# Two-layer trunk on one core: fourteen chunks of the down projection as seven block products per pair, placed between the gate/up chunks

## Chip, core and metric

The kernel runs on one core of one Trainium2 chip. The time is device microseconds of one launch; several runs are timed and their median is given. Smaller is better.

## What is computed

A trunk of two layers on 256 tokens with 1024 features, in float32. Each layer is a gated token mixer and a SwiGLU feed-forward part, each followed by a LayerNorm of the scaled residual. The change lies in the feed-forward part:

```python
def swiglu(x, w_gate, w_up, w_down):
    return (jax.nn.silu(x @ w_gate) * (x @ w_up)) @ w_down

for l in range(DEPTH):                       # DEPTH = 2
    mix = hybrid_mixer(x, w_in[l], w_branch_sb[l], w_branch_moba[l], w_out[l])
    x = layer_norm(DEEPNORM_ALPHA * x + mix, ln_mix_g[l], ln_mix_b[l])
    ffn = swiglu(x, w_ffn_gate[l], w_ffn_up[l], w_ffn_down[l])
    x = layer_norm(DEEPNORM_ALPHA * x + ffn, ln_ffn_g[l], ln_ffn_b[l])
```

The hidden width is 2816, which is 22 chunks of 128. h is silu(gate) times up.

## The kernel before

**Precision by parts.** Every float32 operand is split into a rounded part `hi` and a rest `lo` (`x - hi`), and each product is three matmuls (`mm3`): hi by hi, hi by lo, lo by hi.

**Weights.** `WeightStream` brings the weights as granules of 128 x 1024 in the order in which TensorE uses them, 122 per layer (`NG_LAYER`). A granule is loaded by SyncE's queue into one of six `raw` buffers (`NRAW`), ScalarE casts it to `whi`, VectorE subtracts to `wlo`. Both parts go to rings of ten places (`NSPLIT`): granule g takes the place of g - 10, and `allow` lets it be written once TensorE is done with that. Seven granules per layer, all in the mixer (`SOFT_IN_LAYER`), go another way and are called soft: POOL's queue starts a rounding DMA straight into `whi` (`cast_line`), ScalarE writes its negative into `wlo`, and POOL's queue starts a DMA that adds the weights to it (`rest_line`).

**Feed-forward part.** In a layer granules 56 to 63 are gate and up for chunks 0 to 3, computed with the tokens as rows (`pft`, `h_line`). Granules 64 to 99 are gate and up for chunks 4 to 21, two per chunk (`feat_major`, tiles `pf`, 48 matmuls of 256 columns per chunk), into two PSUM banks in turn; after each chunk ScalarE and VectorE make h and split it (`swiglu_line`, tile `sf`). Granules 100 to 121 are the down projection, one per chunk (`token_out`, tiles `pd`, in layer 1 also `pe`): for each of two token blocks and two halves of 512 columns an `mm3`. Its first 14 chunks run for both token blocks, the last 8 (`HOLD`) first for one and then for the other, so that the first block's norm runs beside the second block's chunks.

**Order.** TensorE's order is that of the code. What ScalarE, VectorE and the queues do between is put in order while the program is written: `Weave` keeps an estimated clock for each engine, and side lines (`line`, `cast_line`, the h lines, the norms) are continued when their due time has come. Each engine then works through its list in that order and waits where an operand isn't there. `SOFT_LAND` is the landing time that this planner assumes for a soft granule.

Of the kernel before, what the change touches and what calls it, by code (L numbers as in the profile page):

```python
# [14 lines left out]
P = 128  # L15
# [15 lines left out]
NG_LAYER = 122  # L31
NTOK_FC = 4


# [65 lines left out]
class WeightStream:  # L100
# [5 lines left out]
    def __init__(self, nc, pool, rings, w, total, weave):  # L106
        self.nc, self.pool, self.rings, self.w, self.total, self.weave = nc, pool, rings, w, total, weave
        self.soft = [g for g in range(total) if SOFT(g)]
        self.hard = [g for g in range(total) if not SOFT(g)]
        self.loaded = self.split = self.cast = self.done = 0  # L110
        self.limit = NSPLIT - 1
# [7 lines left out]
    def open(self, g):  # L119

        self._open(g)
        self.parts[g] = [self._part(i, g) for i in range(2)]
        self.ready[g] = 0.0
        self.loaded = self.split = g + 1
# [4 lines left out]

    def moved(self, start, dst, g, **kw):  # L130

        b, i = divmod(g % NG_LAYER - 40, 4)
        if 0 <= b < 2:
            g += i - 4 * b
            start(dst.rearrange("p (c n) -> p c n", c=2),
                  self.w[g:g + 2, :, b * 512:(b + 1) * 512].rearrange("c p n -> p c n"), **kw)
        else:
            start(dst, self.w[ORDER.get(g, g)], **kw)

    def load(self, upto):  # L140

        while self.loaded < min(upto, len(self.hard)):
            g = self.hard[self.loaded]
            before = self.hard[self.loaded - NRAW] if self.loaded >= NRAW else None
            self._open(g)
            self.moved(self.nc.sync.dma_start, self.raw[g], g)
            self.dma_t = max(self.dma_t, self.ready.get(before, 0.0) + 0.5) + 1.46
            self.there[g] = self.dma_t + 1.0
            self.loaded += 1

    def _part(self, i, g):


        at = g % NSPLIT * GCOLS + (ON[i] if self._on(g) else 0)
        return self.rings[i][:, at:at + GCOLS]

    def _on(self, g):
        return any(a <= g < b for a, b in STATIONARY)

    def line(self):  # L160

        nc, weave = self.nc, self.weave
        while self.split < len(self.hard):
            g = self.hard[self.split]
            ahead = g - self.current
# [6 lines left out]
            self.load(self.split + NRAW)  # L172
            if ahead > 0:
                yield self.there[g]
            hi, lo = (self._part(i, g) for i in range(2))
            t = self.raw.pop(g)
            e = weave.act(self.there[g], GCOLS, nc.scalar.copy, hi, t)
            if g - self.current > 0:
                yield e
            e = weave.dve(e, GCOLS, nc.vector.tensor_sub, lo, t, hi.bitcast(F32))  # L180
            self.parts[g], self.ready[g] = (hi, lo), e
            self.split += 1
            self.load(self.split + NRAW)

    def cast_line(self):
        nc, weave = self.nc, self.weave
        while self.cast < len(self.soft):
# [6 lines left out]
            self.dma_t = max(self.dma_t, e + 1.0) + 2.2  # L194
            self.there[g] = self.dma_t + SOFT_LAND[self.weave.measured]
            self.cast += 1
# [23 lines left out]
    def allow(self, g):  # L220

        reaches = self._on(g) and not self._on(g - NSPLIT + 1) and g % NSPLIT < NSPLIT - 1
        self.limit = max(self.limit, min(g - reaches, self.total - 1))

# [22 lines left out]
NRAW = 6  # L247
SOFT_IN_LAYER = (22, 25, 28, 31, 34, 37, 40)


def SOFT(g):
    return g % NG_LAYER in SOFT_IN_LAYER


NSPLIT = 10
ON = (16, 48)
STATIONARY = ((8, 20), (24, 50), (64, 100), (130, 140), (146, 170), (186, 220))
HOLD = 8
TURNED = ("l0sb3", "l1sb3")
# [18 lines left out]
def hybrid_trunk_kernel(ctx: ExitStack, tc: tile.TileContext, w, xT_in, x_in, ln_in,  # L278
# [39 lines left out]
    def turn(e):  # L318

        was = None  # L320
        while True:
# [5 lines left out]
            else:  # L327
# [5 lines left out]
             for p, n, on in ((ring0, "whi", ON[0]), (ring1, "wlo", ON[1]))]  # L333
    ws = WeightStream(nc, wpool, rings, w, DEPTH * NG_LAYER, weave)
    act, dve, pool = weave.act, weave.dve, weave.pool
# [445 lines left out]

    def residual(e, x, cs, ps, sum_out=None):
        return dve(e, cs.stop - cs.start, nc.vector.scalar_tensor_tensor, x[:, cs], x[:, cs], ALPHA, ps,
                   op0=OP.mult, op1=OP.add, accum_out=sum_out)

# [9 lines left out]

    def norm_line(name, t, junk, gb):

# [27 lines left out]
    def last_norm(name, t, banks, gb, down):  # L825
# [8 lines left out]
        for i, (c0, ps) in enumerate(banks):  # L834
            if t == 1:
                down([(c0, ps)])
            residual(pe_done(), x, cols[i], ps)
            e = dve(0.0, cols[i].stop - c0, nc.vector.bn_stats, st[:, i, :], x[:, cols[i]])
# [16 lines left out]
    for l in range(DEPTH):  # L855
        G = l * NG_LAYER
        L = f"l{l}"
# [185 lines left out]
        hb = [unit(f"{L}hb{t}", [P, 2, 2, 256]) for t in range(2)]  # L1043
        h_t = [pair_tiles(f"{L}h0", [P, 4, S])]

        def h_parts(c):
            if c // 4 == len(h_t):
                h_t.append(pair_tiles(f"{L}h{c // 4}", [P, 4, S]))
            return h_t[c // 4][0][:, c % 4, :], h_t[c // 4][1][:, c % 4, :]

        def h_line(name, ps, j, t):
            sg = work.tile([P, 256], F32, tag="T", name=name)
            e = act(pe_done(), 256, nc.scalar.activation, sg, ps[:, :256], AF.Sigmoid)
            yield e
            dve(e, 256, nc.vector.tensor_mul, sg, sg, ps[:, :256])
# [3 lines left out]
            yield from split_line(*(blocked(h[:, 2 * j:2 * j + 2, ts]) for h in h_t[0]), tp, 256, e)  # L1059

        def swiglu_line(name, ps, hi, lo):
            sg = work.tile([P, S], F32, tag="T", name=name)
            e = act(pe_done(), S, nc.scalar.activation, sg, ps[:, 0, :], AF.Sigmoid)
            yield e
            dve(e, S, nc.vector.tensor_mul, sg, sg, ps[:, 0, :])
            e = dve(e, S, nc.vector.tensor_mul, sg, sg, ps[:, 1, :])
            yield e
            yield from split_line(hi, lo, sg, S, e)

        sides = []  # L1070
        for t in range(2):
            weave.finish(norms[:t + 1])
            pe_after(xT_ready[t])
            for j in range(2):
# [6 lines left out]
                sides.append(weave.start(h_line(f"{L}sg{t}{j}", ps, j, t)))  # L1081
        for c in range(NTOK_FC, NFC):
            ps = bankM(f"{L}pf{c}", [P, 2, S])
            for b in range(2):
                feat_major(ps[:, b, :], G + 56 + 2 * c + b)
            weave.start(swiglu_line(f"{L}sf{c}", ps, *h_parts(c)))
        weave.finish(sides)


        gb = load_gb(l, 1)  # L1090
        acc = [bankB(f"{L}pd{t}", [P, 2, 512]) for t in range(2 if l < DEPTH - 1 else 1)]
        banks = [[(512 * h, a[:, h, :]) for h in range(2)] for a in acc]
        if l == DEPTH - 1:
            banks.append([(0, bankM(f"{L}pe0", [P, 512])), (512, bankM(f"{L}pe1", [P, 512])[:, :256]),
                          (768, bankC(f"{L}pe2", [P, 512])[:, :256])])
        g = G + 100
        for c in range(NFC - HOLD):
            for t in range(2):
                token_out(banks[t], g + c, t, *h_parts(c), c == 0, False)
            ws.allow(g + NSPLIT + c)  # L1100
        norms = []
        for t in range(2):
            def down(part, t=t):
                for c in range(NFC - HOLD, NFC):
                    token_out(part, g + c, t, *h_parts(c), False, c == NFC - 1)
                    if t == 1:
                        ws.allow(g + NSPLIT + c)
            if l < DEPTH - 1:
                down(banks[t])
                norms.append(weave.start(norm_line(f"{L}b", t, acc[t], gb)))  # L1110
            else:
                last_norm(f"{L}b", t, banks[t], gb, down)
# [86 lines left out]
```

## Time and profile before

| | |
|---|---|
| runs timed | 718.47, 719.17, 720.03 us; median 719.17 us |
| span of the profiled execution | 716.7 us; a time of its own beside the span is not listed |
| TensorE (PE) busy | 708.0 us, 99%; mean clock granted 0.997 |
| VectorE (DVE) busy | 528.3 us, 74% |
| ScalarE (ACT) busy | 389.3 us, 54% |
| GpSimd (POOL) busy | 34.6 us, 5% |
| DMA | 157.84 MB, mean 220 GB/s |
| layer 0, gate/up chunks 4 to 21 | 198.1 to 296.0 us |
| layer 0, down projection | 296.0 to 356.9 us |
| layer 1, gate/up chunks 4 to 21 | 549.9 to 648.2 us |
| layer 1, down projection and last norm | 648.2 us to the end |

PE is the matmul unit, PEld its weight loads, which overlap. Names such as `whi<-raw` read output from input. Most instructions are recorded at a helper's line (L442 matmuls, L49 ScalarE, L54 VectorE, L59 POOL), so that tiles tell more than lines. Square brackets in a timeline hold the engine's idle time before an instruction and what ended it. Matmuls are pipelined: one lasts longer in the trace than the distance to the next.

### The profile page before, as it was taken

The page shows a single profiled execution, that of the slowest core. Times are in us where ns is not written, and L with a number is a line of the kernel's source. Part 1 is how long each engine was busy: PE and PEld are TensorE (multiplying, and loading weights), DVE is VectorE, ACT ScalarE, POOL GpSimd, SP SyncE. Part 2 cuts the span into 40 slices and gives each one's busy share as a digit, 9 for nine tenths or more (in the row PEclk, how much of TensorE's full clock was granted, in tenths as well). Part 3 has the DMA queues.
Part 4 walks back from the last instruction along what each step waited for, and adds up shares of the span by engine and source line. Part 5 has one row for each costly group of instructions (what it writes and reads, how often), then busy time and mean ns, then how long its engine had stood idle before and what let it go on. Part 6 is the DMA issues. An engine that isn't in the chain of part 4 may idle for free.

```text
span 716.7 us, 12727 instructions
## 1 busy us (share of the span) xinstructions
PE 708.0 (99%) x4981; PEld 651.0 (91%) x4981; DVE 528.3 (74%) x789; ACT 389.3 (54%) x582; POOL 34.6 (5%) x48
## 2 busy tenths in 40 slices
PE   9999999999999999999999999999999999999995
PEld 7889999998899999988889889999888999998885
DVE  5999887898987666643688888879889776665416
ACT  5766677754655545432365567676556554554300
POOL 0001110001000000000000111100010000000001
PEclk9999999999999999999999999999999999999998
DMA  8898889876596555385259589996748855553501
GB/s 291 342 332 248 244 235 252 288 272 228 197 306 231 181 204 196 128 313 187 85 175 347 160 218 242 242 292 207 260 166 282 302 185 196 191 202 99 225 1 59
DMA packets 63053, 157.84 MB, mean 220 GB/s; under 512 B 10896, under 2 KB 23184, under 8 KB 62992
## 3 DMA queue, kind: packets, MB, share of 16 engines
q1 hardware_dynamic: 58304, 142.07, 57.3%
q0 software_dynamic: 4544, 14.68, 9.0%
q8 instruction: 39, 0.64, 0.4%
q10 hardware_dynamic: 144, 0.26, 0.1%
q14 instruction: 22, 0.18, 0.1%
HBM read 148.87 MB, written 8.13 MB: 219 GB/s over the span
## 4 chain that ended last, share of the span: by engine, by line
PE 97%; DMA 1%; SPq 1%; DVE 0%; POOL 0%; POOLq 0%; issue 0%; ACT 0%; DVEq 0%
PE l1pf L442 14%; PE l0pf L442 14%; PE l0pd L442 8%; PE l0pg L442 6%; PE l1pg L442 6%; PE l1pe L442 4%; PE l1pd L442 4%; PE l1pqk L442 3%; PE l1pft L442 3%; PE l0pqk L442 3%; PE l0pw L442 3%; PE l1pvq L442 3%; PE l0pft L442 3%; PE l1pw L442 3%; PE l1pk L442 2%; PE l0pk L442 2%
## 5 line engine op out<-in xcount | busy, mean ns | idle before, releaser
L54 DVE TENSOR_TENSOR wlo<-raw,whi 128x1024 fp32r<-128x1024 f32 (+1 forms) x234 | 277.2, 1202 | 79.6 <-ACT whi L49 76.5
L49 ACT CAST whi<-raw 128x1024 fp32r<-128x1024 f32 (+1 forms) x233 | 237.5, 1036 | 81.5 <-PE l0pd L442 19.4
L442 PE MATMUL l1pf<-xT_hi,whi 128*128 128x256 f32 x288 | 79.6, 276 | 0.0
L442 PE MATMUL l1pf<-xT_hi,wlo 128*128 128x256 f32 x288 | 79.6, 276 | 0.0
L442 PE MATMUL l1pf<-xT_lo,whi 128*128 128x256 f32 x288 | 79.6, 276 | 0.0
L442 PE MATMUL l0pf<-xT_hi,wlo 128*128 128x256 f32 x288 | 79.5, 276 | 0.0
L442 PE MATMUL l0pf<-xT_hi,whi 128*128 128x256 f32 x288 | 79.5, 276 | 0.0
L442 PE MATMUL l0pf<-xT_lo,whi 128*128 128x256 f32 x288 | 79.5, 276 | 0.0
L442 PEld LDWEIGHTS l1pf<-xT_lo,whi 128*128 128x128 f32 x288 | 54.1, 188 | 0.0
L442 PEld LDWEIGHTS l1pf<-xT_hi,whi 128*128 128x128 f32 x288 | 54.1, 188 | 0.0
L442 PEld LDWEIGHTS l1pf<-xT_hi,wlo 128*128 128x128 f32 x288 | 54.1, 188 | 0.0
L442 PEld LDWEIGHTS l0pf<-xT_lo,whi 128*128 128x128 f32 x288 | 54.1, 188 | 0.0
L442 PEld LDWEIGHTS l0pf<-xT_hi,whi 128*128 128x128 f32 x288 | 54.1, 188 | 0.0
L442 PEld LDWEIGHTS l0pf<-xT_hi,wlo 128*128 128x128 f32 x288 | 54.1, 188 | 0.0
L442 PE MATMUL l0pg<-xT_hi,whi 128*128 128x256 f32 x128 | 35.7, 279 | 0.0
L442 PE MATMUL l1pg<-xT_hi,whi 128*128 128x256 f32 x128 | 35.6, 278 | 0.0
L442 PE MATMUL l0pg<-xT_hi,wlo 128*128 128x256 f32 x128 | 35.4, 277 | 0.0
L442 PE MATMUL l0pg<-xT_lo,whi 128*128 128x256 f32 x128 | 35.4, 277 | 0.0
L442 PE MATMUL l1pg<-xT_hi,wlo 128*128 128x256 f32 x128 | 35.4, 277 | 0.0
L442 PE MATMUL l1pg<-xT_lo,whi 128*128 128x256 f32 x128 | 35.4, 276 | 0.0
L442 PE MATMUL l0pd<-whi,l0h_hi 128*128 128x512 f32 x88 | 34.5, 391 | 0.0
L442 PE MATMUL l0pd<-wlo,l0h_hi 128*128 128x512 f32 x88 | 34.3, 389 | 0.0
(371 smaller groups left out, 1781.5 us busy)
## 6 DMA issues: line engine op xcount, KB each, us to landing
raw<-in_w_dram SPq DMA_DIRECT2D x226, 512.0 KB, 4.5
whi<-in_w_dram POOLq DMA_DIRECT2D x14, 512.0 KB, 6.2
wlo<-in_w_dram POOLq DMA_DIRECT2D x14, 512.0 KB, 8.2
ln<-in_ln_dram SPq DMA_DIRECT2D x8, 512.0 KB, 6.0
raw<-in_w_dram SPq DMA_DIRECT2D x7, 256.0 KB, 5.8
l0mb_scr<-l0mb_turn SPq DMA_DIRECT2D x4, 384.0 KB, 7.2
l0mb_turn<-l0mb_scr SPq DMA_DIRECT2D x16, 96.0 KB, 5.3
l1mb_scr<-l1mb_turn SPq DMA_DIRECT2D x4, 384.0 KB, 6.3
```

Of the source, the lines that this page charges most:

```text
L49: f(*args, **kw)
L54: f(*args, **kw)
L442: nc.tensor.matmul(o, a, b, start=start, stop=stop)
```

## The change

Chunks 4 to 17 of the down projection become seven pairs. A pair's work is a product of 2 x 2 blocks (two token blocks by two chunks, two chunks by two halves of the output columns), and it is done by seven block products in place of eight, with sums of blocks of h and of the weights made beforehand. Seven sums of products stay in PSUM over all pairs: `p1`, `p5`, `p6`, `p7` and three halves of `acc`. After pair 6 `combine_line` adds and subtracts them into x on VectorE, with the residual's factor; the norm then adds the tail's sums with factor 1.

Pair j (chunks 4+2j and 5+2j) stands between gate/up chunks: products with its first two granules, then gate/up chunk 8+2j, the other products, chunk 9+2j. Chunks 4 to 7 come ahead of pair 0, so h of a pair is made two pairs ahead. From chunk 8 on gate/up uses one PSUM bank (`single`, half of `acc[1]`) instead of two, since the products hold the others. Chunks 0 to 3 and 18 to 21 (`TAIL`) stay as before and come last, first for one token block and then for the other.

A pair has four weight granules from two loads: B11 (half a granule: the first 512 columns of the first raw buffer), B2X (the second raw buffer whole), T13 and T42 (sums made in place in the two raw buffers by four VectorE adds of 512 columns). A layer has 136 granules instead of 122; pair j has the eight granules 72+8j to 79+8j: B11, B2X, gate and up of a chunk, T13, T42, gate and up of the next. The up granule 75+8j is soft: seven more soft granules per layer, and the planner's landing time for them is 6 us. Silu replaces Sigmoid and a multiply, and ScalarE copies the up part from PSUM.

```diff
+NPROD = 7
+NS_LAYER = NG_LAYER + 2 * NPROD
+LEAD_FC = NTOK_FC + 4
+TAIL = [*range(NTOK_FC), *range(NTOK_FC + 2 * NPROD, NFC)]
...
-SOFT_IN_LAYER = (22, 25, 28, 31, 34, 37, 40)
+SOFT_IN_LAYER = (22, 25, 28, 31, 34, 37, 40, *(59 + 2 * LEAD_FC + 8 * j for j in range(NPROD)))
...
+            if kind == B11:
+                t = t[:, :512]
+            elif kind == T13:
+                u = self.raw[of + 1]
+                a, b = (slice(i * 512, (i + 1) * 512) for i in range(2))
+                dve = weave.dve
+                dve(max(e, self.there[of + 1]), 512, add, t[:, a], t[:, a], t[:, b])
+                e = dve(0.0, 512, add, t[:, b], t[:, b], u[:, b])
+            n = t.shape[1]
+            e = weave.act(e, n, nc.scalar.copy, hi, t)
+            if kind == T13:
+                dve(0.0, 512, add, u[:, b], u[:, b], t[:, a])
+                self.there[of + 1] = dve(0.0, 512, add, u[:, a], u[:, a], u[:, b])
...
+        def activated(name, ps):
+            both = work.tile([P, 512], F32, tag="T", name=name)
+            act(pe_done(), S, nc.scalar.activation, both[:, :S], ps[:, 0, :], AF.Silu)
+            e = act(pe_done(), S, nc.scalar.copy, both[:, S:], ps[:, 1, :])
+            return both, e
...
+        def product(o, j, h, w, i):
+            hi, lo = h_pair[j % 3]
+            cs = slice(i * 512, (i + 1) * 512)
+            mm3(o, hi[:, h, :], lo[:, h, :], w[0][:, cs], w[1][:, cs], j == 0, j == NPROD - 1 and h in (0, 2, 6, 7))
...
+        for j in range(NPROD):
+            weave.finish(made[2 * j:2 * j + 2])
+            pe_after(h_there[j])
+            w = ws.take(g)
+            product(p1, j, 0, w, 0)
+            ws.allow(g + NSPLIT)
+            w = ws.take(g + 1)
+            product(acc[0][:, 0, :], j, 4, w, 0)
+            product(acc[0][:, 1, :], j, 3, w, 1)
+            ws.allow(g + 1 + NSPLIT)
+            h_chunk(LEAD_FC + 2 * j, single, g + 2)
+            w = ws.take(g + 4)
+            product(p5, j, 6, w, 0)
+            product(p7, j, 2, w, 1)
+            ws.allow(g + 4 + NSPLIT)
+            w = ws.take(g + 5)
+            product(acc[1][:, 0, :], j, 5, w, 0)
+            product(p6, j, 7, w, 1)
+            ws.allow(g + 5 + NSPLIT)
+            if j == NPROD - 1:
+                combined = [weave.start(combine_line())]
+            h_chunk(LEAD_FC + 2 * j + 1, single, g + 6)
+            g += 8
...
-        for c in range(NFC - HOLD):
-            for t in range(2):
-                token_out(banks[t], g + c, t, *h_parts(c), c == 0, False)
-            ws.allow(g + NSPLIT + c)
```

**ScalarE in layer 0, around chunks 8 and 9.** The number behind `raw` is the granule; `l0sf8` is chunk 8's tile. Before, a chunk has one activation, its h cast and two weight casts:

```order
L49 ACTIVATE l0sf8_2628<-l0pf8_2563 128x256
L49 CAST whi_98<-raw83_2459 128x1024
L49 CAST l0h2_hi_2626<-l0sf8_2628 128x256
L49 CAST whi_98<-raw84_2476 128x1024
L49 ACTIVATE l0sf9_2691<-l0pf9_2630 128x256
L49 CAST whi_98<-raw85_2523 128x1024
L49 CAST l0h2_hi_2626<-l0sf9_2691 128x256
L49 CAST whi_98<-raw86_2541 128x1024
```

Now, beginning with T13 of the next pair (granule 84, in buffer `raw80`); `raw81` is granule 85, T42, and the activation from `whi` to `wlo` is the negation of soft granule 83:

```order
L54 CAST whi_98<-raw80_2283 128x1024
L54 ACTIVATE l0sf8_2645<-l0pd1_2564 128x256
L54 COPY l0sf8_2645<-l0pd1_2564 128x256
L54 CAST whi_98<-raw81_2424 128x1024
L54 CAST whi_98<-raw86_2458 128x1024
L54 CAST whi_98<-raw87_2488 128x1024
L54 ACTIVATE wlo_99<-whi_98 128x1024
L54 CAST whi_98<-raw88_2535 128x512
L54 ACTIVATE l0sf9_2731<-l0pd1_2564 128x256
L54 COPY l0sf9_2731<-l0pd1_2564 128x256
L54 CAST whi_98<-raw89_2655 128x1024
L54 CAST l0hp2_hi_2291<-l0sf8_2645 128x512
```

The negation stands behind the casts of granules 86 and 87; the activation and the copy of a chunk now read the one bank (`l0pd1`) that the next chunk writes.

**VectorE at the same place.** Before, a chunk has two multiplies with a PSUM operand and one subtraction of 256 columns beside two granules:

```order
L54 TENSOR_TENSOR wlo_99<-raw82_2407,whi_98 128x1024
L54 TENSOR_TENSOR l0sf8_2628<-l0sf8_2628,l0pf8_2563 128x256 x2
L54 TENSOR_TENSOR wlo_99<-raw83_2459,whi_98 128x1024
L54 TENSOR_TENSOR l0h2_lo_2627<-l0sf8_2628,l0h2_hi_2626 128x256
L54 TENSOR_TENSOR wlo_99<-raw84_2476,whi_98 128x1024
```

Now, from chunk 11 to the first granules after chunk 12:

```order
L59 TENSOR_TENSOR l0sf11_2894<-l0sf10_2811,l0sf11_2894 128x256
L59 TENSOR_TENSOR l0sf10_2811<-l0sf11_2894 128x128
L59 TENSOR_TENSOR wlo_99<-raw97_2794,whi_98 128x1024
L59 TENSOR_TENSOR l0hp0_lo_2288<-l0sf10_2811,l0hp0_hi_2287 128x512
L59 TENSOR_TENSOR l0hp0_lo_2288<-l0sf11_2894,l0hp0_hi_2287 128x512
L59 TENSOR_TENSOR wlo_99<-raw98_2830,whi_98 128x1024
L59 TENSOR_TENSOR raw96_2701<-raw96_2701 128x512
L59 TENSOR_TENSOR raw96_2701<-raw96_2701,raw97_2794 128x512
L59 TENSOR_TENSOR raw97_2794<-raw97_2794,raw96_2701 128x512
L59 TENSOR_TENSOR raw97_2794<-raw97_2794 128x512
L59 TENSOR_TENSOR wlo_99<-raw96_2701,whi_98 128x1024
L59 TENSOR_TENSOR l0sf12_2974<-l0sf12_2974 128x256
```

The four adds of raw weights and the sums of h are new in the list; nothing of a chunk's h reads PSUM any more.

**POOL in layer 0 after the mixer.** Before, nothing but the norms' small operations:

```order
L59 TENSOR_TENSOR l0a_ve1_2091<-l0a_ve1_2091,mhalf_105 128x1
L59 TENSOR_SCALAR l0b_ve0_3743<-l0b_ve0_3743 128x1
L59 TENSOR_TENSOR l0b_ve0_3743<-l0b_ve0_3743,mhalf_105 128x1
L59 TENSOR_SCALAR l0b_ve1_3834<-l0b_ve1_3834 128x1
L59 TENSOR_TENSOR l0b_ve1_3834<-l0b_ve1_3834,mhalf_105 128x1
```

Now the first of seven times two DMAs stand there:

```order
L64 TENSOR_TENSOR l0a_ve1_2091<-l0a_ve1_2091,mhalf_105 128x1
L146 DMA whi_98<-in_w_dram 128x1024
L146 DMA wlo_99<-in_w_dram 128x1024
L146 DMA whi_98<-in_w_dram 128x1024
L146 DMA wlo_99<-in_w_dram 128x1024
```

Each pair's rounding DMA is issued behind the adding DMA of the pair ahead of it.

More of the change, by code (lines that the diff above doesn't have):

```diff
@@ L109, in __init__ @@
         self.hard = [g for g in range(total) if not SOFT(g)]
+        self.loads = [g for g in self.hard if SLOTS[g][0] in (FULL, B11, B2X)]
         self.loaded = self.split = self.cast = self.done = 0
+        self.freed = {}
         self.limit = NSPLIT - 1
@@ L128, in load_piece, with moved @@
         self.dma_t += 0.73
-    def moved(self, start, dst, g, **kw):
+    def moved(self, start, dst, slot, **kw):
+        g = SLOTS[slot][1]
         b, i = divmod(g % NG_LAYER - 40, 4)
@@ L138, in moved, with load @@
             start(dst, self.w[ORDER.get(g, g)], **kw)
[L140 to L144, printed above, removed]
+    def load(self, upto=None):
+        while self.loaded < min(upto or len(self.loads), len(self.loads)):
+            g = self.loads[self.loaded]
+            before = self.loads[self.loaded - NRAW] if self.loaded >= NRAW else None
+            if before is not None and before not in self.freed:
+                break
             self._open(g)
             self.moved(self.nc.sync.dma_start, self.raw[g], g)
-            self.dma_t = max(self.dma_t, self.ready.get(before, 0.0) + 0.5) + 1.46
+            self.dma_t = max(self.dma_t, self.freed.get(before, 0.0) + 0.5) + 1.46
             self.there[g] = self.dma_t + 1.0
@@ L151, in _part, with _place @@
     def _part(self, i, g):
[L154 to L158, printed above, removed]
+        kind = self._place(g)
+        at = g % NSPLIT * GCOLS + (ON[i] if kind == "on" else HALF_AT if kind == "half" else 0)
+        return self.rings[i][:, at:at + (512 if kind == "half" else GCOLS)]
+    def _place(self, g):
+        if SLOTS[g][0] == B11:
+            return "half"
+        if SLOTS[g][0] == B2X:
+            return "off"
+        return "on" if any(a <= g < b for a, b in STATIONARY) else "off"
     def line(self):
         nc, weave = self.nc, self.weave
+        add = nc.vector.tensor_add
         while self.split < len(self.hard):
             g = self.hard[self.split]
+            kind = SLOTS[g][0]
             ahead = g - self.current
@@ L171, in line @@
                 continue
-            self.load(self.split + NRAW)
-            if ahead > 0:
+            self.load()
+            of = g - 4 if kind in (T13, T42) else g
+            if ahead > 0 and of == g:
                 yield self.there[g]
             hi, lo = (self._part(i, g) for i in range(2))
-            t = self.raw.pop(g)
-            e = weave.act(self.there[g], GCOLS, nc.scalar.copy, hi, t)
+            t = self.raw[of]
+            e = self.there[of]
+            if kind == B11:
[11 more added lines that the diff above has]
+                self.there[of + 1] = dve(0.0, 512, add, u[:, a], u[:, a], u[:, b])
             if g - self.current > 0:
                 yield e
-            e = weave.dve(e, GCOLS, nc.vector.tensor_sub, lo, t, hi.bitcast(F32))
+            e = weave.dve(e, n, nc.vector.tensor_sub, lo, t, hi.bitcast(F32))
             self.parts[g], self.ready[g] = (hi, lo), e
+            if kind in (FULL, T13, T42):
+                self.raw.pop(of)
+                self.freed[of] = e
             self.split += 1
-            self.load(self.split + NRAW)
+            self.load()
     def cast_line(self):
@@ L220, in allow @@
     def allow(self, g):
-        reaches = self._on(g) and not self._on(g - NSPLIT + 1) and g % NSPLIT < NSPLIT - 1
-        self.limit = max(self.limit, min(g - reaches, self.total - 1))
+        g = min(g, self.total - 1)
+        reaches = self._place(g) == "on" and self._place(g - NSPLIT + 1) == "off" and g % NSPLIT < NSPLIT - 1
+        self.limit = max(self.limit, g - reaches)
     def reach(self, g):
@@ new lines, in hybrid_trunk_kernel, with combine_line @@
+        taken[0] += 2
+        p1, p6 = (bankC(f"{L}pd{n}", [P, 512]) for n in ("one", "six"))
+        p5, p7 = (bankM(f"{L}pd{n}", [P, 512]) for n in ("five", "seven"))
+        def combine_line():
+            e = pe_done()
+            u = work.tile([P, 512], F32, tag="T", name=f"{L}comb")
+            e1 = act(e, 512, nc.scalar.copy, u, p1)
+            e = residual(e, xs[0], halves[0], p1)
+            left[turns[0]] = max(e, e1)
+            yield e1
+            left[turns[1]] = e = dve(e1, 512, nc.vector.tensor_add, u, u, p6)
+            residual(e, xs[0], halves[1], u, op=OP.subtract)
+            residual(e, xs[0], halves[1], p5, scale=1.0)
+            yield weave.dve_t + HOP
+            e = dve(e, 512, nc.vector.tensor_sub, u, u, p7)
+            residual(e, xs[1], halves[0], u)
+            yield weave.dve_t + HOP
+            residual(e, xs[1], halves[1], u, op=OP.subtract)
+            residual(e, xs[1], halves[1], p5, scale=1.0)
@@ L1101, in hybrid_trunk_kernel, with h_parts @@
+        def h_parts(i):
+            return [h[:, i % 4, :] for h in (h_tok, h_rest)[i // 4]]
         norms = []
```

119 lines of the change are left out of this document (80 added, 39 removed).

## The prediction

> **What bounds the kernel now.** I read the page's totals first, then the chain that ended last in order of time, then the busy time by stretches.
>
> ```profile
> span 716.7 us, 12727 instructions
> PE 708.0 (99%) x4981; PEld 651.0 (91%) x4981; DVE 528.3 (74%) x789; ACT 389.3 (54%) x582; POOL 34.6 (5%) x48
> PE 97%; DMA 1%; SPq 1%; DVE 0%; POOL 0%; POOLq 0%; issue 0%; ACT 0%; DVEq 0%
> ...
> 198.09 97.94 PE l0pf L442 x864
> 296.03 55.79 PE l0pd L442 x246
> ...
> 549.92 98.26 PE l1pf L442 x864
> ...
> 198.10:296.00 97.90, 97.90 (x865) 97.90 (x865) 68.46 (x96) 51.51 (x76) 0.00 (x0) 1.00 0.62 219
> ```
>
> TensorE carries 97% of the chain. Its pieces in layer 0's gate/up stage (l0pf) and down stage (l0pd) join without a gap. So whatever leaves TensorE's list is gained, and whatever makes TensorE wait is lost, one for one. A 256-column matmul costs 97.94/864 = 0.1134 us there, a 512-column one 55.79/246 = 0.2268 us, the same per column. The last row has the columns PE, PEld, DVE, ACT, POOL, clock, DMA share, GB/s: the clock is at 1.00, VectorE busy 70%, ScalarE 53%. The time outside the span is not listed for this execution; the runs' median, 719.17, is 2.5 above the span, and I keep that.
>
> **TensorE's sum.** Two chunks of the down projection cost 2 x 2 tokens x 2 halves x 3 = 24 matmuls of 512 columns. Seven products cost 21. Seven pairs in two layers save 7 x 2 x 3 = 42 x 0.2268 = 9.53 us. Chunks 0-3 and 18-21 keep 12 each, and gate/up keeps its count. The end of layer 1 keeps its last pieces (eight chunks, half by half), so nothing is lost there.
>
> **VectorE and ScalarE in a pair.** One pair's period on TensorE is 96 x 0.1134 + 21 x 0.2268 = 15.65 us. The prices are distances between starts, since neighbours overlap by some 0.1 us:
>
> ```profile
> 214.88 0.88 DVE L54 TENSOR_TENSOR l0sf<-l0sf,l0pf 128x256 f32<-128x256 f32 x2 [0.90 <-ACT l0sf L49]
> 215.82 1.23 DVE L54 TENSOR_TENSOR wlo<-raw,whi 128x1024 fp32r<-128x1024 f32 x1
> 216.96 0.42 DVE L54 TENSOR_TENSOR l0h_lo<-l0hb,l0h_hi 128x256 fp32r<-128x256 f32 x1
> ...
> 353.44 0.68 DVE L54 TENSOR_TENSOR xT_lo<-l0b_tp,xT_hi 128x512 fp32r<-128x512 f32 x1
> 354.04 1.22 DVE L54 TENSOR_TENSOR wlo<-raw,whi 128x1024 fp32r<-128x1024 f32 x1
> ...
> 369.37 0.29 DVE L54 TENSOR_TENSOR l1qmb_ra<-l1qmb_tok,rope 128x128 f32<-128x128 f32 x1 [1.08 <-ACT l1qmb_tok L49]
> ...
> 214.47 0.38 ACT L49 ACTIVATE l0sf<-l0pf 128x256 f32<-128x256 f32 x1 [1.74 <-PE l0pf L442]
> 214.75 1.04 ACT L49 CAST whi<-raw 128x1024 fp32r<-128x1024 f32 x1
> 215.69 0.40 ACT L49 CAST l0h_hi<-l0hb 128x256 fp32r<-128x256 f32 x1
> ```
>
> VectorE: six subtractions of 1024 columns at 1.14 (215.82 to 216.96) = 6.84; half a granule 0.60; the four adds of raw weights, each reading the one before, at their full 0.68 = 2.72; the h lines with two multiplies of 256 at 0.42, one subtraction of 256 at 0.42, two of 128 at 0.29, two of 512 at 0.60 = 3.04. Sum 13.2 of 15.65, 84%. ScalarE: six casts at 0.94 = 5.64, half a cast 0.5, a negation 0.94, two Silus and two copies at 0.28 = 1.1, two casts of 512 at about 0.5: 9.2, 59%. Neither is the bound, and both have slack for in-order waiting: by the order shown, a cast for granule g waits for TensorE to leave granule g-10, so weights stand up to ten granules ahead, as before:
>
> ```profile
> ACT whi L49 <- PE l0pd L442: 19.4, 13, 1.7
> ACT whi L49 <- PE l0pf L442: 12.5, 16, 0.9
> ACT l0sf L49 <- PE l0pf L442: 32.6, 18, 1.8
> ```
>
> ScalarE waits for TensorE, not the reverse; that cover hides the new vector work. The combination after pair 6 is eight VectorE passes of 512 at 0.61, 4.9 us; it stands beside chunk 21's 5.44 us and 10.9 us of the tail before the norm reads x. I cost it at nothing. Without that cover it would cost its 4.9 us once in each layer, since the norm reads x.
>
> **Raw buffers.** A pair keeps two of the six raw buffers until its sums are split, so the load of granule 89 waits for VectorE's subtraction of 84, whose cast stands just ahead of chunk 8's Silu; granule 89's own cast stands behind chunk 9's copy. Between lie granules 76 to 79, 1.36 + 1.36 + 5.44 = 8.2 us, less about 1.9 for that subtraction, plus 0.7 for Silu and copy: 7 us of room.
>
> ```profile
> raw<-in_w_dram SPq DMA_DIRECT2D x226, 512.0 KB, 4.5
> ```
>
> The median landing is 4.5, so I take 0; what comes later than 7 would first eat the slack of the next paragraph.
>
> **The single bank.** From chunk 8 on, gate/up writes one bank instead of two. After an odd chunk TensorE has 9 products (2.04 us) before it writes the bank again, after an even one 12 (2.72 us). ScalarE needs Silu and copy, 2 x 0.28 plus 0.1 to start and 0.1 to end, about 0.8. Slack is 1.2 us in the tighter place, provided that no 0.94 us cast started just before; the last row says that ScalarE has so far arrived 1.8 us early. Between 0 and 0.9 per chunk (28 chunks), I take 0.
>
> **The soft granule.** One gate/up granule per pair comes by a rounding DMA (whi), a negation on ScalarE and an adding DMA (wlo), all on POOL's queue. In layer 0 it is granule 83 (75 + 8j). By the order the negation stands behind the cast of granule 87, which waits for TensorE to leave 77. From there TensorE has granules 78 and 79 (5.44), 80 (3 products, 0.68), 81 (6, 1.36), 82 (2.72), and two matmuls before wlo is read (0.23): 10.43 us. Spent before the DMA: 0.1, the cast 0.94, the negation 1.06, and 0.30 to POOL's issue (436.52 to 436.82):
>
> ```profile
> 435.46 1.06 ACT L49 ACTIVATE wlo<-whi 128x1024 fp32r<-128x1024 f32 x1
> ...
> 436.82 0.87 POOL L138 DMA_DIRECT2D wlo<-in_w_dram  x1 [1.86 <-ACT wlo L49]
> ...
> DMA to landing us min/median/max: 5.2/8.2/9.8
> ...
> wlo<-in_w_dram POOLq DMA_DIRECT2D x1, 512.0 KB, 5.4
> ...
> wlo<-in_w_dram POOLq DMA_DIRECT2D x1, 512.0 KB, 7.9
> ```
>
> So 10.43 - 2.4 leaves 8.0 us for a landing whose fourteen cases took 5.2 to 9.8, median 8.2 (the third row is of all wlo DMAs; then the one at 426.74, with hardly another transfer beside it, and the one at 85.23, with 1.3 MB of loads beside it). In the pair loop the five raw loads of a pair are issued as VectorE frees their buffers, bunched between its subtractions of 84 and 87, so three or four (1.5 to 2 MB) are under way with wlo. That is nearest to the 7.9 and to the median. I take the median: 0.2 us late. It counts for ten pairs (in pairs 1-5; pair 0 has its granule asked for earlier, in pair 6 the negation stands one cast earlier, room 9.0): 10 x 0.2 = 2.0 us. Bounds: 5.2 costs nothing; 9.8 costs 10 x 1.8 + 2 x 0.8 = 19.6. The first DMA, whi, has from granule 81's end to the negation, 9 us against the same landings.
>
> The Trainium skill (DMA: Bandwidth & Descriptors, Queues, rings and completion order) says that a DMA engine takes the queues it has work for in turn, a packet of some nine or more descriptors at a time; a wlo would then wait for about one load ahead of it and fit its room, and the sum would be 2.0 us lower. The 9.8 in the trace, twice the quiet time, speaks for less than that.
>
> **Table loads.** Silu instead of Sigmoid adds three loads, ahead of l0sg, l1sb_keep and l1sg, none with a wait of its own:
>
> ```profile
> 90.64 1.28 ACT L49 ACT_TABLE_LOAD   x1 [2.65 <-DVE l0mb_nmax L54]
> ...
> 180.83 0.38 ACT L49 ACTIVATE l0sg<-l0pft 128x256 f32<-128x256 f32 x1 [2.61 <-PE l0pft L442]
> ...
> 394.92 0.81 ACT L49 ACTIVATE l1sb_keep<-l1sb_s 128x768 f32<-128x768 f32 x1 [2.33 <-DVE l1sb_s L54]
> ...
> 532.53 0.38 ACT L49 ACTIVATE l1sg<-l1pft 128x256 f32<-128x256 f32 x1 [0.97 <-PE l1pft L442]
> ```
>
> 1.28 fits into 2.61 and 2.33 of idle time and overruns 0.97 by 0.3, on work that TensorE doesn't wait for next: 0, at most 0.3. The Trainium skill (ScalarE: Activation LUTs, What ACT_TABLE_LOAD costs) adds a drain of about 1.38 us to every switch; by that up to 1.7 us would show at l1sg alone. The trace has the next instruction 0.02 us behind the load (91.94), so I leave it out.
>
> **Sum.** 716.7 - 9.5 + 2.0 = 709.2 of span, 711.7 as timed. The smallest change that a measurement of this kernel can tell is about 0.2%, 1.4 us.
>
> **Rivals.**
> - Everything fits, landing at 8.0 or under: 719.17 - 9.53 = 709.6. For it the quiet 5.4 and the 62% DMA share of the stage; I put it in one case with mine (up to 8.4: 713.6), 0.57.
> - wlo lands in 8.4 to 9.0: 4 to 10 us of stalls, 713.6 to 719.6. For it the loads bunched beside it; 0.20, two thirds still faster.
> - The adding DMA decides the sign: from 9.1 on the stalls (10 x 1.1 + 2 x 0.1 = 11.2) exceed the gain by over 0.2%; at 9.5, 15 + 1 = 16 us, 725.6. For it the 9.8; against it, those landings had small packets of other transfers beside them; 0.10.
> - The single bank stalls: ScalarE late by half a cast (0.5) beyond its slack at one chunk in two, 14 x 0.5 = 7 us, 716.7. Against it the early arrivals; 0.07.
> - VectorE becomes the bound: if its chained adds cost so much more that 13.2 became 16.5 us, 14 x 0.85 = 12 us, 721.5. Against it the 70% now and prices from rows of the same stage; 0.06.
>
> **Numbers.** Faster by over 0.2% (under 717.7): 0.57 + 0.14 + 0.06 = 0.77; within: 0.06 from the second and 0.01 from the fourth case, 0.07; slower: 0.10 + 0.06 = 0.16. The range reaches from 708.6 (everything fits, 1 us for the pace) to 721, and leaves out the upper half of the two slow cases and a little below. The first case alone is 709 to 713.6.
>
> **What would show it.** TensorE's matmul count falls by 84: 42 saved ones of 512 columns, and 42 times two of 256 columns in layer 1 that become one of 512. One piece without gaps per pair would show that all fits; gaps in TensorE's row just ahead of the third matmul of granules 83, 91 and so on, released by the wlo DMA, would show the second term, gaps at a chunk's first matmul released by ScalarE the single bank. VectorE's busy share in the pair loop should be near 84 to 90%. Wrong would be: a wlo landing far from 8, or gaps in layer 1's mixer, whose POOL order shifts.

## The result and the profile after

The changed kernel takes 726.0 us (median of four runs, 725.17 to 728.47) against 719.49 us (718.47 to 720.03) of the kernel before on the same chip: 1.0099 times as long, 95% interval 1.0084 to 1.0114. The forecast was 711.7. It is slower by 0.99%, where 1% less was expected.

The page's totals, the chain and the DMA issues of the changed kernel:

```profile
span 723.1 us, 12732 instructions
...
PE 704.0 (97%) x4897; PEld 643.4 (89%) x4897; DVE 581.7 (80%) x873; ACT 426.6 (59%) x651; POOL 54.6 (8%) x76
...
PE 59%; issue 31%; DMA 3%; POOL 2%; DVE 2%; SPq 1%; POOLq 0%; ACT 0%; DVEq 0%
...
raw<-in_w_dram SPq DMA_DIRECT2D x212, 512.0 KB, 5.1
whi<-in_w_dram POOLq DMA_DIRECT2D x28, 512.0 KB, 5.0
wlo<-in_w_dram POOLq DMA_DIRECT2D x28, 512.0 KB, 8.8
```

TensorE has its 84 matmuls fewer (4981 to 4897), but it no longer carries the chain from end to end: 97% before, 59% now. In the pair loops the chain now runs over POOL's DMAs; most of the 31% of "issue" is the time between POOL's instructions there, and not time that TensorE lost (it is busy 97% of the span). What TensorE waits for stands in the view of waits (engine and line, released by; us in total, times, longest):

```profile
PE l0pd L487 <- DMA wlo<-in_w_dram: 4.6, 5, 1.6
PE l1pd L487 <- DMA wlo<-in_w_dram: 3.1, 4, 1.0
PE l1pd L487 <- DVE x L59: 1.6, 1, 1.6
```

To see where the time went I cut both runs at the same three places: first matmul of `l0pft`, first of `l1pvq` (layer 1's mixer), first of `l1pft`, last matmul. The windows of before and then of after (stretch, length, busy PE, PEld, DVE, ACT, POOL, clock, DMA share, GB/s):

```profile
175.20:356.70 181.50, 181.50 (x1242) 167.09 (x1241) 118.00 (x159) 86.58 (x117) 3.37 (x4) 1.00 0.57 203
356.70:526.90 170.20, 170.20 (x1224) 156.23 (x1223) 143.76 (x230) 107.66 (x171) 13.84 (x18) 1.00 0.78 236
526.90:708.90 182.00, 182.00 (x1298) 169.72 (x1297) 113.93 (x155) 79.19 (x108) 3.39 (x4) 1.00 0.51 178
```

```profile
175.00:359.10 184.10, 179.52 (x1220) 164.16 (x1219) 144.47 (x201) 104.33 (x151) 13.41 (x18) 1.00 0.72 221
359.10:530.60 171.50, 171.21 (x1224) 156.58 (x1224) 143.86 (x230) 109.06 (x172) 13.86 (x18) 1.00 0.78 233
530.60:714.60 184.00, 179.31 (x1235) 164.70 (x1234) 140.76 (x197) 97.28 (x142) 13.31 (x18) 1.00 0.65 196
```

Each feed-forward part should have become 4.76 us shorter. Layer 0's became 2.6 longer, layer 1's 2.0; the mixer between them, which the change doesn't touch, became 1.3 longer (1.24 between the starts themselves). The span is 6.4 us longer where 9.5 less was to be had: 15.9 us to find. I took the distances between the starts of TensorE's matmuls, subtracted 0.1134 us per 256 columns, and sorted what was left. A gap comes out about 0.16 us longer this way than in the view of waits, which counts from the modelled end of the matmul ahead, and two short gaps are too short for that view:

| where | us |
|---|---|
| eleven gaps ahead of a soft granule's third matmul, released by `wlo` | 9.5 |
| the first matmul behind each of these gaps, 0.11 slower | 1.2 |
| one gap ahead of a piece of layer 1's last norm, with its restart | 1.8 |
| layer 1's mixer | 1.2 |
| slower matmuls elsewhere in the feed-forward parts | 1.7 |
| from the last matmul to the end, less an earlier start | 0.5 |

The largest entry in one pair of layer 0, from the timelines of ScalarE, SyncE's queue, POOL and TensorE:

```profile
247.32 1.05 ACT L54 CAST whi<-raw 128x1024 fp32r<-128x1024 f32 x1 [0.23 <-PE l0pdsix L487]
248.28 1.05 ACT L54 ACTIVATE wlo<-whi 128x1024 fp32r<-128x1024 f32 x1
247.44 2.60 SPq L146 DMA_DIRECT2D raw<-in_w_dram  x3
249.62 0.86 POOL L146 DMA_DIRECT2D wlo<-in_w_dram  x1 [11.11 <-ACT wlo L54]
257.53 0.28 PE L487 MATMUL l0pd<-xT_lo,whi 128*128 128x256 f32 x1
259.42 0.39 PE L487 MATMUL l0pd<-xT_hi,wlo 128*128 128x256 f32 x1 [1.61 <-DMA wlo<-in_w_dram]
```

ScalarE's cast of granule 87 waits for TensorE, the negation stands behind it, POOL issues the adding DMA at 249.62, and TensorE wants `wlo` at 257.64. The room, from the issue of the adding DMA to the moment at which TensorE wants its data, is 8.0 us, as worked out beforehand; the landing took 9.8. Over the six pairs of the window 228 to 325 it was (minimum, median, maximum)

```profile
DMA to landing us min/median/max: 8.3/8.9/9.8
```

What the DMA does in that time is seen by cutting out the stretch from its issue to its own first packet, 249.6 to 254.4 (queue: packets, MB, share of the 16 engines):

```profile
q1 hardware_dynamic: 320, 1.18, 94.1%
q0 software_dynamic: 1, 0.00, 0.6%
```

In these 4.8 us the DMA engines work almost only on SyncE's queue (q1): on the three raw loads that VectorE's three subtractions in a row had just released (the 247.44 row). Not all of that is waiting in line: an adding DMA with hardly a load beside it (the one at 426.74 before) has its first packet after 1.6 us. Of the 1.1 MB ahead of the first packet here 0.76 MB moved after those 1.6 us; over pairs 1 to 5 of both layers it was 0.49 to 0.78 MB, one load to one and a half.

The other end of the landing has company too. POOL issues the rounding DMA of the next pair 5.5 us behind the adding one, on the same queue, while that is still under way (POOL's row, then the queues from 249.6 to 259.4):

```profile
255.15 0.56 POOL L146 DMA_DIRECT2D whi<-in_w_dram  x1 [4.66 <-PE l0pd L487]
q1 hardware_dynamic: 371, 1.32, 51.6%
q0 software_dynamic: 282, 1.03, 43.1%
```

The adding DMA is 0.52 MB of the 1.03. In the same ten pairs the next rounding DMA moved 0.2 to 0.5 MB before the adding one had landed. No run here takes it away alone.

### The profile page after: what moved, and what is told of

The parts are those of the page before. It is cut to its first block, busy times and chain, and to the rows that moved or that the text cites. A ratio compares the mean times of both kernels' runs of the same rounds, so it can differ in the third digit from the quotient of the medians.

```text
span 723.1 us, 12732 instructions
## 1 busy us (share of the span) xinstructions
PE 704.0 (97%) x4897; PEld 643.4 (89%) x4897; DVE 581.7 (80%) x873; ACT 426.6 (59%) x651; POOL 54.6 (8%) x76
## 4 chain that ended last, share of the span: by engine, by line
PE 59%; issue 31%; DMA 3%; POOL 2%; DVE 2%; SPq 1%; POOLq 0%; ACT 0%; DVEq 0%
PE l1pg L487 6%; PE l0pg L487 6%; PE l0pd L487 6%; PE l1pd L487 5%; PE l0pqk L487 3%; PE l0pw L487 3%; PE l1pqk L487 3%; PE l1pvq L487 3%; PE l1pw L487 3%; DMA wlo<-in_w_dram 2%; PE l1pb L487 2%; PE l1pk L487 2%; PE l0pk L487 2%; PE l0pu L487 2%; PE l1pa L487 2%
## 5 line engine op out<-in xcount | busy, mean ns | idle before, releaser
L487 PE MATMUL l0pd<-xT_hi,wlo 128*128 128x256 f32 x224 | 62.6, 279 | 4.6 <-DMA wlo<-in_w_dram 4.6
L487 PE MATMUL l1pd<-xT_hi,wlo 128*128 128x256 f32 x224 | 62.8, 280 | 3.1 <-DMA wlo<-in_w_dram 3.1
L487 PE MATMUL l1pd<-xT_hi,whi 128*128 128x256 f32 x224 | 62.1, 277 | 0.0
L487 PE MATMUL l1pd<-xT_lo,whi 128*128 128x256 f32 x224 | 62.1, 277 | 0.0
L487 PE MATMUL l0pd<-xT_hi,whi 128*128 128x256 f32 x224 | 62.1, 277 | 0.0
L487 PE MATMUL l0pd<-xT_lo,whi 128*128 128x256 f32 x224 | 62.0, 277 | 0.0
L487 PEld LDWEIGHTS l0pd<-xT_hi,wlo 128*128 128x128 f32 x224 | 42.1, 188 | 5.6 <-DMA wlo<-in_w_dram 5.6
L487 PEld LDWEIGHTS l1pd<-xT_hi,wlo 128*128 128x128 f32 x224 | 42.1, 188 | 4.3 <-DMA wlo<-in_w_dram 4.1
L487 PEld LDWEIGHTS l1pd<-xT_lo,whi 128*128 128x128 f32 x224 | 42.2, 188 | 0.6
L487 PEld LDWEIGHTS l1pd<-xT_hi,whi 128*128 128x128 f32 x224 | 42.1, 188 | 0.6
```

Of the source, the lines that this page charges most:

```text
L487: nc.tensor.matmul(o, a, b, start=start, stop=stop)
```

## Experiments

All times are compared with the kernel before by the ratio of runs on the same chip; the changed kernel's ratio is 1.0099.

**No soft granules in the pairs.**

```
-SOFT_IN_LAYER = (22, 25, 28, 31, 34, 37, 40, *(59 + 2 * LEAD_FC + 8 * j for j in range(NPROD)))
+SOFT_IN_LAYER = (22, 25, 28, 31, 34, 37, 40)
```

> All granules of the pairs come as raw loads with a cast and a subtraction; the seven split-by-DMA granules per layer in the pair loop are gone. Theory A (the late adding DMA is the main loss): the ten gaps at the third matmul of granules 83, 91 and so on (9.4 us in the trace) and the slow restart behind each (0.11 each, 1.2 us) go, 726.0 - 10.6 = 715.4 us, VectorE at 13.2 + 1.14 = 14.3 of 15.65 us in a pair (92%). Rival B (VectorE or the raw buffers take over, with six loads and 92% in a pair): new gaps released by VectorE's wlo, at least half the gain lost, 720.7 us or more. Rival C (the gaps only mark a loss that sits elsewhere): within 1 us of 726.

Measured: 719.62 us, ratio 1.0006 (0.9995 to 1.0018), 6.7 us less than the change. The gaps for `wlo` are gone, others came, all six in layer 0. The wait:

```profile
PE l0pd L487 <- ACT l0sf L54: 4.8, 6, 1.0
```

and ScalarE's timeline ahead of one of them:

```profile
244.78 1.05 ACT L54 CAST whi<-raw 128x1024 fp32r<-128x1024 f32 x1 [2.89 <-DVE raw L59]
245.73 0.37 ACT L54 ACTIVATE l0sf<-l0pd 128x256 f32<-128x256 f32 x1
```

The cast of T13 waits 2.89 us for VectorE's adds, and the Silu and the copy that read the single bank stand behind it in ScalarE's list. So it is neither theory's number. The soft granules are the main loss, and they also buy something: with one subtraction more per pair VectorE's adds come so late that ScalarE's reading of the single bank stalls TensorE. VectorE is not the bound by its sum (layer 1, with the same work, has no such gap; why not is not shown).

The matmul that waits is not the next gate/up chunk. ScalarE's copy and TensorE's rows:

```profile
246.01 0.36 ACT L54 COPY l0sf<-l0pd 128x256 f32<-128x256 f32 x1
245.28 0.40 PE L487 MATMUL l0pdseven<-whi,l0hp_lo 128*128 128x512 f32 x1
246.42 0.50 PE L487 MATMUL l0pd<-whi,l0hp_hi 128*128 128x512 f32 x1 [0.75 <-ACT l0sf L54]
```

It is the product behind `p7`, which writes the first half of `acc[1]` and starts 0.05 us after the copy of the second half, `single`, has ended. `single` itself is written again only six matmuls, 1.36 us, later. So two halves of one tile are waited for as one, as at the end of layer 1 (the bank experiment below); with a tile of its own for `single` this gap should go, which was not run.

**The negation earlier.**

```
-            self.there[g] = self.dma_t + SOFT_LAND[self.weave.measured or g % NS_LAYER > 64]
+            self.there[g] = self.dma_t + (PAIR_LAND if g % NS_LAYER > 64 else SOFT_LAND[self.weave.measured])
+PAIR_LAND = 3.0
```

> The negation of the pair's soft granule is planned 3 us earlier (a constant of the planner, 3.0 for 6.0): on ScalarE it stands right behind the even chunk's copy, ahead of the casts of 85, 86 and 87. Theory A: the adding DMA is issued about 3.2 us earlier, room 8.0 becomes 11.2, no gap is left, 726.0 - 10.6 = 715.4 us; and since it then stands ahead of the three raw loads that VectorE's subtractions release at 247.4, 248.6 and 249.7, its first packet comes 1.5 to 2.5 us after the issue instead of 4.4 and it lands after 6 to 7 us. Rival A2: the loads collide with it all the same, it lands after about 9, which fits too: the same time, another landing. Rival B (the casts of 85 to 87 come a microsecond later and TensorE, or the raw loads, wait for that): 719 to 726.

Measured: 716.02 us, ratio 0.9956 (0.9941 to 0.9971): 10.3 us less than the change, and faster than the kernel before. What is left of the wait in layer 0:

```profile
PE l0pd L488 <- DMA wlo<-in_w_dram: 0.3, 2, 0.2
```

and the landings in the same window as above:

```profile
DMA to landing us min/median/max: 7.5/8.0/9.3
```

Theory A holds for the time, A2 for the landing. It still takes 8.0, since the negation comes only 1 to 2.8 us earlier (room 9.0 to 10.8, 8.3 in the last pair) and the loads follow it closely: 0.5 MB ahead of its first packet and 0.7 to 1.5 beside the rest, in place of 0.9 to 1.1 and 0.1 to 0.65. That is more of SyncE's loads in all (1.2 to 2.0 MB for 1.2 to 1.5), and yet it lands earlier; what left its side is the next rounding DMA, which in nine of the ten pairs moves next to nothing (at most 0.02 MB) before the landing. The landing hardly fell; the room grew past it.

**The second DMA without adding.**

```
-            e = weave.pool(e, self.moved, nc.gpsimd.dma_start, lo, g, accum_op=OP.add)
+            kw = {} if g % NS_LAYER > 64 else dict(accum_op=OP.add)
+            e = weave.pool(e, self.moved, nc.gpsimd.dma_start, lo, g, **kw)
```

> The second DMA of the pairs' soft granules writes instead of adding (wlo then holds the rounded weight and not the rest: this leaves out the addition); its bytes, its place in the queue and its issue stay. Theory D (the landing of 9 us is a wait of 4.4 us behind loads that are queued ahead, where a quiet one has 1.5, and then 3.9 us of adding, where the rounding DMA takes 2.2): the first packet still 4.4 us after the issue, landing 4.4 + 2.2 + 0.5 = 7.1, under the room of 8.0, so hardly a gap, about 715.5 us. Rival E (the loads beside it set it all): landing still 8.5 to 9, time within 1.5 us of 726.

Measured: 715.33 us, ratio 0.9946 (0.9927 to 0.9966), 11.0 us less than the change, by a landing under the room:

```profile
DMA to landing us min/median/max: 7.0/7.3/8.4
```

The time and the landing came about as theory D said (two pairs of layer 0 still landed late), but not by its parts: the first packet came after 2.3 to 3.2 us instead of 3.6 to 4.7, and from first to last packet it still took about 4 to 5, with 0.6 to 0.75 MB of loads beside it. By the medians adding costs about 1.6 us of the 8.9. Part of that is the loads' place: without the stalls the last of the three comes 0.8 us behind the DMA's issue, and 0.1 in the changed kernel. In pair 1 of each layer they lie alike in both runs, and there the landing falls from 9.2 to 8.1 and from 8.7 to 7.3, so adding is worth 1.1 to 1.4.

**Half the bytes beside it.**

```
+            if SLOTS[g][0] == FULL and 72 <= g % NS_LAYER < 128:
+                half = slice(0, 512)
+                self.nc.sync.dma_start(self.raw[g][:, half], self.w[SLOTS[g][1], :, half])
...
+                t = t[:, None, :512].to_broadcast([P, 2, 512])
```

> The changed kernel with the raw loads of the pairs' gate and up granules (three of the five loads of a pair) cut to half their bytes; casts and subtractions read that half twice, so that the list and the lengths on every engine stay (this leaves out half of those weights). Theory Q (the adding DMA lands late because 1.2 MB of loads stand ahead of it, and 0.3 MB beside): about 0.8 MB instead of 1.5, first packet 3 us after the issue instead of 4.3, landing 7.2 to 7.8 instead of 8.9, under the room of 8.0: the gaps go, 715.4 us. Rival (the adding DMA is slow by itself, whatever runs beside it): landing still 8.5 to 9, within 1.5 us of 726.

Measured: 717.58 us, ratio 0.9976 (0.9962 to 0.9990), 8.8 us less than the change:

```profile
DMA to landing us min/median/max: 7.3/7.9/9.0
```

With 0.8 to 1.0 MB of loads in place of 1.2 to 1.5 the landing falls from 8.9 to 7.9, to the edge of the room; four late ones are left (0.2 to 1.0 us, 2.3 in all), the two largest with 0.6 and 0.8 MB ahead of their first packet. Theory Q holds in its direction; the landing stayed a little above the 7.2 to 7.8 expected, and the time 2.2 us above. Together with the run before: alone the adding DMA took 5.4 us, the transfers beside it make it 8.9, and without the adding it takes 7.3 beside about the same loads. Taking away the adding brings most landings under the room, taking away a third of the loads' bytes brings them to its edge.

The packet records of the changed kernel and of the five runs in which the pairs' DMA still adds and the loop has 512-column products put this together: the landing goes with all bytes that move beside it until it lands, those of POOL's own queue counted. With 1.2 to 1.5 MB the middle landing was 7.8 us (18 landings in the pair loops), with 1.5 to 1.7 MB 8.5 (28), with more 9.0 (25). A longer landing also counts more bytes, so part of this is only the counting.

**A bank of its own for a piece of the last norm.**

```
-            banks[1][1:] = [(512, single[:, 0, :]), (768, bankC(f"{L}pe", [P, 512])[:, :256])]
+            banks[1][1:] = [(512, bankM(f"{L}pe0", [P, 512])[:, :256]), (768, bankC(f"{L}pe", [P, 512])[:, :256])]
```

> In the last norm of layer 1 the second token block's third quarter (columns 512 to 767) goes to a bank of its own instead of the half of a tile whose other half VectorE still reads. Theory: the wait of 1.55 us ahead of that piece (released by VectorE's x) and its restart 0.12 go, 726.0 - 1.7 = 724.3 us. Rival: VectorE, which is busy with the first token block's scaling until then, is late anyway and the end moves by less than 0.5 us: 725.5 to 726.

The gap in the timeline of the changed kernel, VectorE's row and TensorE's rows around it:

```profile
708.16 0.68 DVE L59 SCALAR_TENSOR_TENSOR x<-x,l1pd 128x512 f32<-128x512 f32 x1
706.95 0.39 PE L487 MATMUL l1pd<-whi,l1hr_lo 128*128 128x512 f32 x1
708.89 0.38 PE L487 MATMUL l1pd<-whi,l1h_hi 128*128 128x256 f32 x1 [1.55 <-DVE x L59]
```

and the same place with the separate bank:

```profile
707.54 0.39 PE L487 MATMUL l1pd<-whi,l1hr_lo 128*128 128x512 f32 x1
707.76 0.28 PE L487 MATMUL l1pe<-whi,l1h_hi 128*128 128x256 f32 x1
```

Measured: 723.84 us, ratio 1.0069 (1.0048 to 1.0090), 2.2 us less than the change. `single` is the second half of the tile `acc[1]`. TensorE's new piece writes that half, but waits until VectorE has read the first half, and VectorE gets to that only after the first token block's scaling (it ends at 708.2). With another tile the wait isn't there. So the program waited for more than the data need: what TensorE writes and what VectorE reads are different halves.

**Both.** The early negation and the separate bank together.

> The early negation and the separate bank together. If the two losses are independent, 716.0 less the 1.7 us of the last wait, 714.3 us, 4.3 us under the kernel before as it ran in that comparison (718.6). Rival: VectorE becomes the last to finish and hides part of it, 715 to 716.

Measured: 714.82 us, ratio 0.9935 (0.9919 to 0.9951). The losses add up: 1.5 us less than with the early negation alone.

**The place of ten granules in the ring.** The table's entry now reaches to slot 189: over the four granules of `l1pb` (180 to 183) and over six of `l1pw` behind them.

```
-STATIONARY = ((8, 20), (24, 50), (64, 130), (144, 180), (200, 260))
+STATIONARY = ((8, 20), (24, 50), (64, 130), (144, 190), (200, 260))
```

> As the run with both, and the ring's shifted placement of layer 1's granules reaches to slot 189 instead of 179, so that the last four granules of the branch products (slots 180 to 183, l1pb) lie as the others do. Theory: their 96 matmuls of 256 columns, which the trace has at 0.120 us apart in the changed kernel and at 0.1134 in the one before, go back to 0.1134: 96 x 0.0066 = 0.6 us, 713.7 us. Rival: the 0.120 comes from something else in that place (the other transfers, the order of the list): no change, 714.3.

The rows of `l1pb` in the changed kernel and here (duration minimum, median, maximum in ns; first and last start):

```profile
L487 PE MATMUL l1pb<-l1omb_hi,whi x32: 283/283/283, 496.3 to 507.5; 128*128 128x256 f32 x32
```

```profile
L488 PE MATMUL l1pb<-l1omb_hi,whi x32: 276/276/277, 491.0 to 501.5; 128*128 128x256 f32 x32
```

Measured: 713.19 us, ratio 0.9915 (0.9900 to 0.9931), the fastest version here, 0.85% under the kernel before. The 96 matmuls are back at 0.1134 us apart from 0.1200, 0.63 us, by a shift of 16 and 48 elements of the weights they load. The timed difference to the run before, 1.4 us, has an interval wider than itself, so the 0.6 is shown by the trace alone. It isn't all gained: the matmuls of `l1pw` whose granules are now shifted too became 0.24 us slower in all, so the mixer is 0.42 us shorter than in the run before.

The rest of the mixer's 1.2 us is a wait that the kernel before does not have, in the view of waits of the changed kernel:

```profile
PE l1pg L487 <- DVE l1vmb L59: 0.3, 1, 0.3
```

TensorE's first matmul of `l1pg` waits for VectorE's multiply of `l1vmb`. By distances between starts that is 0.45 us and 0.11 of restart; 0.29 more stand at a piece of `l1mb_o`, and `l1pqk` is 0.26 shorter. The run without soft granules in the pairs has the same 0.3, so it is not theirs; why VectorE comes late there is not shown.

**One length of matmul.**

```
+            for q in range(2):
+                qs = slice(i * 512 + q * 256, i * 512 + (q + 1) * 256)
+                part = o[:, q * 256:(q + 1) * 256]
+                mm(part, hi[:, h, :], w[0][:, qs], False, False)
...
```

> As e6_place, but pairs 1 to 6 do their products in matmuls of 256 columns, two for one of 512; lists of the other engines are the same. In e6_place a pair without a gap takes 15.78 us on TensorE, where 96 x 0.1134 + 21 x 0.2268 makes 15.65. Theory (each change between products of 512 and chunks of 256 columns slows the matmuls behind it): with one length all through, 15.65 a pair, 12 x 0.13 = 1.6 us less, 711.6 us. Rival 1 (the extra 0.13 belongs to the weights' place in the ring, not to the length): 15.78 as before, 713.2. Rival 2 (twice the weight loads for the same columns cost something): more than 15.78, slower than 713.2.

Measured: 714.98 us, ratio 0.9947 (0.9933 to 0.9960), 2.3 us more than with 512 columns. A pair takes 15.93 us, not 15.65: the theory falls, and the time is as rival 2 said. Its cause, the weight loads, is not shown by that. Many of the products' matmuls stand 0.12 apart:

```profile
267.39 0.28 PE L488 MATMUL l0pdone<-whi,l0hp_hi 128*128 128x256 f32 x1
267.51 0.28 PE L488 MATMUL l0pdone<-wlo,l0hp_hi 128*128 128x256 f32 x1
267.63 0.28 PE L488 MATMUL l0pdone<-whi,l0hp_lo 128*128 128x256 f32 x1
```

Over five pairs the products' 42 average 0.1186 and the chunks' 96 average 0.1141: 4.98 + 10.95 = 15.93. So most products run near the slower pace that `l1pb` had without its shift. Their loaded operand is h and not a weight of the ring; whether its place is the reason was not tried. With 512 columns the 0.13 us of a pair are 0.07 in the products (0.22 with 256) and 0.06 in the chunks' matmuls, by the same distances; what makes them stays open.

**Silu in the kernel before.**

```
-            e = act(pe_done(), S, nc.scalar.activation, sg, ps[:, 0, :], AF.Sigmoid)
+            e = act(pe_done(), S, nc.scalar.activation, sg, ps[:, 0, :], AF.Silu)
-            dve(e, S, nc.vector.tensor_mul, sg, sg, ps[:, 0, :])
```

> The kernel before with Silu for Sigmoid and its first multiply in the gate/up lines, so that the table loads of the change are tried alone (and VectorE does one multiply less per chunk). Step 6 of the prediction: hidden, at most 0.3 us, so within 0.5 us of the kernel before. Rival: a drain with each of the added loads, of which 1.7 us would show at l1sg, so 1.5 to 2 us slower.

Measured: 719.47 us against 719.59, ratio 0.9996 (0.9984 to 1.0007): no difference. The load at the place with the least idle time, and what follows it:

```profile
532.94 1.28 ACT L49 ACT_TABLE_LOAD   x1
534.24 0.38 ACT L49 ACTIVATE l1sg<-l1pft 128x256 f32<-128x256 f32 x1
```

## Why the prediction was wrong

**TensorE's sum: right.** 84 matmuls fewer. Where nothing waits (the fastest version, five pairs of layer 0) a pair takes 15.78 us against 15.65 forecast; the row of that stretch has TensorE busy without a break:

```profile
235.80:314.67 78.87, 78.87 (x587) 74.44 (x586) 66.39 (x90) 49.34 (x71) 7.10 (x10) 1.00 0.79 237
```

**VectorE and ScalarE: right.** The same row: VectorE 66.39 / 78.87 = 84%, as forecast; ScalarE 63% for 59%. In the changed kernel TensorE did not wait for the combination, for a raw buffer or for ScalarE's reading of the single bank. The first experiment shows how near the last was, and that its slack was reckoned to the wrong matmul: after an even chunk not 12 matmuls but 6 stand ahead of the one that has to wait, the next into the same tile.

**The soft granule: the step that failed, by its size.** Place, mechanism and room were right: 7.9 to 8.0 us in each of the ten pairs. The landing was taken at 8.2, 2.0 us in all; it was 8.9, and the ten gaps with their restarts came to 10.5. The text had the three bunched loads, and still took the median of fourteen landings from other stages. Sorted by SyncE's loads beside them until the landing, by the packet records, those were of two kinds: of seven with at most 0.7 MB six landed after 5.2 to 7.0 us and one after 8.5; of seven with 0.9 MB or more one landed after 7.9 and six after 8.5 to 9.8. A pair has 1.2 to 1.5 MB of loads; the rows to take were the latter. The next pair's rounding DMA on the same queue had no part in the text at all.

Of the 13.9 us by which the span missed its forecast, 8.7 are this step (10.7 us with the short gap of pair 6 in layer 1, for 2.0). The other 5.2 are terms that the sum had at nothing.

The rule brought against this sum, from the Trainium skill (DMA: Bandwidth & Descriptors, Queues, rings and completion order), was that a DMA engine serves its queues in turn by packets, by which the adding DMA would wait for about one load. These traces do not speak clearly against it: beyond the 1.6 us of a quiet one it waited for one load to one and a half (0.49 to 0.78 MB). What failed is what was drawn from it, that it then fits its room: first packets came after 3.6 to 4.7 us, and landings after 8.2 to 9.8.

**The end of layer 1: "nothing is lost there" failed.** 1.8 us. The piece count was right; that this program waits for two halves of one tile as for one was not looked at, though the move of that piece to `single` stands in the diff.

**Terms that were missing.** A gap costs its length and 0.11 us of restart (1.2 us). In the mixer, `l1pb`'s weights no longer lie at shifted places, since the 14 granules more per layer move layer 1's slots against the table (0.6 us), and most of the rest is the wait for `l1vmb`; a gap there was among the prediction's signs of being wrong. And 1.7 us of slower matmuls in the feed-forward parts had no term; the 0.13 us of each of fourteen pairs would make 1.8.

**The rivals.** The landing itself, 8.9, lies in the second rival (8.4 to 9.0), whose price of 713.6 to 719.6 us fell short by the missing terms. The sign was decided by the adding DMA, as the third said, but its point of 9.1 assumed that nothing else is lost. With the 6.4 us above (1.2, 1.8, 1.2, 1.7 and 0.5 of the table), 9.53 of gain is used up at gaps of 3.1 us in all, a landing of 8.3. Of the other rivals, everything fitting gets the closest look from the fastest version: 713.2 us, 3.6 above its 709.6. The single bank and VectorE as the bound did not come true here.

**Table loads: right.** No difference in time, and the next instruction 0.02 us behind the load (534.24, after 532.94 + 1.28). The drain that the Trainium skill (ScalarE: Activation LUTs, What ACT_TABLE_LOAD costs) adds shows nowhere in that row.

## What to carry to other kernels

Where a transfer's landing decides, don't take a median over stages: sort the landings by the bytes in flight beside them, its own queue's included, and take the row that has as many as the new place will have. A margin of 0.2 us that recurs ten times is a bet; either give the transfer a microsecond of room (here one planner constant, 10 us) or count it as late. When a step reuses the idle half of a tile, or adds entries ahead of a table of positions, look up what is keyed to the tile and to the position.

## What the hardware showed

- An adding DMA of 512 KB, issued with the last of three loads of 512 KB on another queue, moved its first packet after 4.7 us, when 1.1 MB of the others were through; a quiet one needs 1.6 us to that point. Landing: 5.4 us alone, 7.9 with 0.8 to 1.0 MB of loads beside it, 8.9 with 1.2 to 1.5, in both cases with up to 0.5 MB of the next DMA on its own queue; 7.3 in the last case if it writes instead of adding.
- The 96 matmuls of 256 columns of `l1pb` stood 0.120 us apart with their loaded weights unshifted in the ring, and 0.1134 us with a shift of 16 (rounded part) and 48 (rest) elements; six granules of `l1pw`, shifted in the same run, are streamed and not loaded, and their matmuls became 0.24 us slower in all.
- After a gap of 0.1 to 1.8 us in TensorE's row the first matmul stood 0.11 us further from the next than usual, in twelve cases of the changed kernel's feed-forward parts.
